# Batch norm with ReLU on one core: regrouping the last two stores so that one of them spans both halves of x

## Chip, cores and metric

One core of a Trainium2 chip; the seven other cores are idle. The metric is the device time of one execution in microseconds (us), as the median of several executions. The span in a profile is about 1.7 us shorter than the time.

## The reference

```python
x: (32, 128, 32, 32) float32      # 16.78 MB in, 16.78 MB out
gamma, beta, running_mean, running_var: (128,) float32

normalized = (x - running_mean[None, :, None, None]) / np.sqrt(running_var[None, :, None, None] + eps)
scaled = normalized * gamma[None, :, None, None] + beta[None, :, None, None]
return np.maximum(scaled, 0).astype(np.float32)
```

## The kernel before

The 4096 (batch, channel) rows of 1024 numbers are dealt out so that a partition holds 16 neighbouring rows of each of two halves (t = 0 and 1). A row is 4 KB, so a partition's part of one half is 64 KB in one piece of HBM. Loads go out on SyncE's queue, stores on ScalarE's (ACT's). One ACTIVATE does one row: relu(scale * x + bias).

```python
TILES = ((0, 0, 2), (0, 2, 4), (0, 4, 8), (0, 8, 16), (1, 0, 16))   # (half, first row, end)
LOAD_CUTS = {(1, 8)}        # the load of the second half is cut at row 8
STORE_CUTS = {(0, 1)}
...
for t, a, b in TILES:
    xt = data.tile([P, b - a, HW], F32, name=f"x{t}_{a}")
    ...                     # one load per piece, all six queued at once
# ... four small loads of the parameters, scale_t and bias_t computed ...
for t, a, b, xt in tiles:
    first = a
    for j in range(a, b):
        nc.scalar.activation(out=xt[:, j - a, ...], in_=xt[:, j - a, ...], func=ACTF.Relu,
                             bias=bias_t[:, j : j + 1], scale=scale_t[:, j : j + 1])
        if j + 1 == b or (t, j + 1) in STORE_CUTS:
            nc.scalar.dma_start(out=outr[t, :, first : j + 1, :], in_=xt[:, first - a : j + 1 - a, :])
            first = j + 1
```

The stores have 0.5, 0.5, 1, 2, 4 and 8 MB. Nothing is written in a buffer twice, so no load waits for a store.

Of the kernel before, what the change touches and what calls it, by code (L numbers as in the profile page):

```python
# [1 line left out]

# [4 lines left out]


F32 = mybir.dt.float32
ACTF = mybir.ActivationFunctionType  # L10



J = 16

TILES = ((0, 0, 2), (0, 2, 4), (0, 4, 8), (0, 8, 16), (1, 0, 16))

LOAD_CUTS = {(1, 8)}
STORE_CUTS = {(0, 1)}

HALVES = {(0, 0), (0, 1)}


@with_exitstack
def kernel(
    ctx: ExitStack,
    tc: tile.TileContext,
    x: bass.AP,
    gamma: bass.AP,
    beta: bass.AP,  # L30
    running_mean: bass.AP,
    running_var: bass.AP,
    eps: bass.AP,
    out: bass.AP,
):
    nc = tc.nc
    B, C, H, W = x.shape
    HW = H * W
    P = nc.NUM_PARTITIONS
    assert C % J == 0 and P % (C // J) == 0 and (B * C) % (P * J) == 0  # L40
    Q = C // J
    T = B * C // (P * J)

    xr = x.rearrange("b c h w -> (b c) (h w)").rearrange("(t p j) w -> t p j w", p=P, j=J)
    outr = out.rearrange("b c h w -> (b c) (h w)").rearrange("(t p j) w -> t p j w", p=P, j=J)

    data = ctx.enter_context(tc.tile_pool(name="data", bufs=1))
    params = ctx.enter_context(tc.tile_pool(name="params", bufs=1))
    psum = ctx.enter_context(tc.tile_pool(name="psum", bufs=1, space=bass.MemoryType.PSUM))

    tiles = []
    for t, a, b in TILES:
        xt = data.tile([P, b - a, HW], F32, name=f"x{t}_{a}")
        cuts = [a] + [j for j in range(a + 1, b) if (t, j) in LOAD_CUTS] + [b]
        for c, d in zip(cuts, cuts[1:]):
            nc.sync.dma_start(out=xt[:, c - a : d - a, :], in_=xr[t, :, c:d, :])  # L56
        tiles.append((t, a, b, xt))



    raw = params.tile([Q, 4, J], F32, name="raw")
    for k, src in enumerate((running_var, gamma, running_mean, beta)):
        nc.scalar.dma_start(out=raw[:, k, :], in_=src.rearrange("(q j) -> q j", j=J))
    eps_t = params.tile([P, 1], F32, name="eps_t")
    nc.vector.memset(eps_t, float(eps))  # L65
    rep = params.tile([Q, P // Q, Q], F32, name="rep")
    nc.gpsimd.memset(rep, 1.0)  # L67
    nc.gpsimd.affine_select(  # L68
        out=rep,
        in_=rep,  # L70
        compare_op=mybir.AluOpType.is_equal,
        fill=0.0,
        base=0,
        pattern=[[0, P // Q], [-1, Q]],
        channel_multiplier=1,
    )
    cols = psum.tile([P, 4, J], F32, name="cols")
    nc.tensor.matmul(  # L78
        cols.rearrange("p k j -> p (k j)"),
        rep.rearrange("q r s -> q (r s)"),  # L80
        raw.rearrange("q k j -> q (k j)"),
        start=True,
        stop=True,
    )
    std_t = params.tile([P, J], F32, name="std_t")
    nc.scalar.activation(out=std_t, in_=cols[:, 0, :], func=ACTF.Sqrt, bias=eps_t[:, 0:1], scale=1.0)  # L86
    rstd_t = params.tile([P, J], F32, name="rstd_t")
    nc.vector.reciprocal(out=rstd_t, in_=std_t)  # L88
    scale_t = params.tile([P, J], F32, name="scale_t")
    nc.vector.tensor_mul(out=scale_t, in0=cols[:, 1, :], in1=rstd_t)  # L90
    ms_t = params.tile([P, J], F32, name="ms_t")
    nc.vector.tensor_mul(out=ms_t, in0=cols[:, 2, :], in1=scale_t)  # L92
    bias_t = params.tile([P, J], F32, name="bias_t")
    nc.vector.tensor_sub(out=bias_t, in0=cols[:, 3, :], in1=ms_t)  # L94

    with tc.manual_schedule(engines={mybir.EngineType.Activation}):
        for t, a, b, xt in tiles:
            first = a
            for j in range(a, b):
                step = HW // 2 if (t, j) in HALVES else HW  # L100
                for w in range(0, HW, step):
                    nc.scalar.activation(  # L102
                        out=xt[:, j - a, w : w + step],
                        in_=xt[:, j - a, w : w + step],
                        func=ACTF.Relu,
                        bias=bias_t[:, j : j + 1],
                        scale=scale_t[:, j : j + 1],
                    )
                if j + 1 == b or (t, j + 1) in STORE_CUTS:
                    nc.scalar.dma_start(  # L110
                        out=outr[t, :, first : j + 1, :], in_=xt[:, first - a : j + 1 - a, :]
                    )
                    first = j + 1


# [1 line left out]
_INS = ['x', 'gamma', 'beta', 'running_mean', 'running_var', 'eps']  # L117
_OUTS = [((32, 128, 32, 32), 'float32')]

_NUMBERS = {'eps': 1e-05}  # L120


# [26 lines left out]
```

## Time and profile before

| | before |
|---|---|
| time, first three runs | 83.94, 83.65, 83.94 us |
| span of the profile | 82.0 us |
| bytes | 33.56 MB, 1792 packets |
| DMA engines busy | 48.7% by loads + 47.6% by stores |
| ACT busy | 39.1 us (48%) |

How to read it: no other part is as busy as the DMA engines. The prediction below shows the strip, the stretches and the order of the issues. One more group of lines, by line and shape, gives what one row costs; its columns are busy us and mean ns, then the idle time before:

```profile
L102 ACT ACTIVATE x<-x,bias_t,scale_t 128x1024 f32<-128x1024 f32 x30 | 34.5, 1227 | 8.5 <-DMA x<-in_x_dram 7.6 <-ACT x L102 0.9
```

ACT's idle time is mostly waiting for loads (7.6 us). ACT keeps up with the loads and isn't the bound.

### The profile page before, as it was taken

What the parts mean: (1) busy time and instruction counts of PE and PEld (TensorE: products, weight loads), DVE (VectorE), ACT (ScalarE), POOL (GpSimd) and SP (SyncE); (2) the same over time, 40 slices, a digit from 0 to 9 for tenths busy, and PEclk for the clock granted to TensorE, in tenths of its full rate; (3) what the DMA queues carried; (4) which work ended last, traced back from release to release, by engine and by line L of the source; (5) the groups of instructions that cost most, each with busy time, mean ns of one, the idle gap of its engine ahead of it and who ended that gap; (6) DMA issues with size and microseconds to landing.
All of it is one profiled execution on the core that took longest, in us unless ns stands there. A gap on an engine that the chain in (4) does not pass through costs nothing.

```text
span 82.0 us, 120 instructions
## 1 busy us (share of the span) xinstructions
PE 0.7 (1%) x2; PEld 0.5 (1%) x2; DVE 0.8 (1%) x5; ACT 39.1 (48%) x36; POOL 0.8 (1%) x6
## 2 busy tenths in 40 slices
PE   0002000000000000000000000000000000000000
PEld 0002000000000000000000000000000000000000
DVE  0000300000000000000000000000000000000000
ACT  0600477799239999199994199993000000000000
POOL 3000000000000000000000000000000000000000
DMA  2899997979899989999799799998992999996590
GB/s 48 336 424 456 416 544 336 524 322 526 338 434 430 506 358 506 390 434 444 320 460 500 316 424 448 512 432 368 480 736 128 416 512 512 512 512 288 224 512 0
DMA packets 1792, 33.56 MB, mean 409 GB/s; under 512 B 256, under 2 KB 256, under 8 KB 512
## 3 DMA queue, kind: packets, MB, share of 16 engines
q1 hardware_dynamic: 864, 16.78, 48.7%
q10 hardware_dynamic: 928, 16.78, 47.6%
HBM read 16.78 MB, written 16.78 MB: 409 GB/s over the span
## 4 chain that ended last, share of the span: by engine, by line
DMA 56%; ACT 10%; issue 2%; SPq 0%
DMA x<-in_x_dram 56%; ACT x L102 10%; SPq L56 0%
## 5 line engine op out<-in xcount | busy, mean ns | idle before, releaser
L102 ACT ACTIVATE x<-x,bias_t,scale_t 128x1024 f32<-128x1024 f32 (+1 forms) x34 | 37.5, 1177 | 9.9 <-DMA x<-in_x_dram 7.6
L86 ACT ACT_TABLE_LOAD x1 | 1.3, 1283 | 2.6 <-issue 2.6
L86 ACT ACTIVATE std_t<-cols,eps_t 128x16 f32<-128x16 f32 x1 | 0.3, 273 | 4.5 <-PE cols L78 4.5
L78 PE MATMUL cols<-raw,rep 8*128 8x64 f32 x2 | 0.7, 429 | 7.6 <-DMA raw<-in_beta_dram 7.6
L78 PEld LDWEIGHTS cols<-raw,rep 8*128 8x128 f32 x2 | 0.5, 306 | 7.6 <-issue 7.6
L68 POOL TENSOR_SCALAR_AFFINE_SELECT rep<-rep 8x128 f32<-8x128 f32 x1 | 0.4, 392 | 0.1
L88 DVE RECIPROCAL rstd_t<-std_t 128x16 f32<-128x16 f32 x1 | 0.3, 254 | 7.7 <-ACT std_t L86 7.7
L67 POOL MEMSET rep<- 8x128 f32 x1 | 0.2, 194 | 0.3 <-POOLq L130 0.3
L90 DVE TENSOR_TENSOR scale_t<-cols,rstd_t 128x16 f32<-128x16 f32 x1 | 0.2, 175 | 0.1
L92 DVE TENSOR_TENSOR ms_t<-cols,scale_t 128x16 f32<-128x16 f32 x1 | 0.2, 175 | 0.0
L94 DVE TENSOR_TENSOR bias_t<-cols,ms_t 128x16 f32<-128x16 f32 x1 | 0.2, 174 | 0.0
L130 POOL MEMSET const-bfloat16-1.0<- 128x1 bf16 x1 | 0.1, 106 | 0.0
L130 POOL MEMSET const-uint8-127<- 128x1 uint8 x1 | 0.1, 106 | 0.0
L130 POOL MEMSET const-float32-0.0<- 128x1 f32 x1 | 0.1, 103 | 0.3 <-issue 0.3
L130 POOL MEMSET const-float32-1.0<- 128x1 f32 x1 | 0.1, 103 | 0.0
L65 DVE MEMSET eps_t<- 128x1 f32 x1 | 0.1, 59 | 0.9 <-PEq L130 0.9
## 6 DMA issues: line engine op xcount, KB each, us to landing
x<-in_x_dram SPq DMA_DIRECT2D x3, 4096.0 KB, 38.7
out_dram<-x ACTq DMA_DIRECT2D x1, 4096.0 KB, 28.7
x<-in_x_dram SPq DMA_DIRECT2D x2, 1024.0 KB, 5.8
x<-in_x_dram SPq DMA_DIRECT2D x1, 2048.0 KB, 11.3
out_dram<-x ACTq DMA_DIRECT2D x1, 2048.0 KB
out_dram<-x ACTq DMA_DIRECT2D x2, 512.0 KB, 19.6
out_dram<-x ACTq DMA_DIRECT2D x1, 1024.0 KB
raw<-in_running_var_dram ACTq DMA_DIRECT2D x1, 0.5 KB
```

Source lines behind the costliest of these rows:

```text
L65: nc.vector.memset(eps_t, float(eps))
L67: nc.gpsimd.memset(rep, 1.0)
L68: nc.gpsimd.affine_select(out=rep, in_=rep, compare_op=mybir.AluOpType.is_equal, fill=0.0, base=0, pattern=[[0, P // Q], [-1, Q]], channel ...
L78: nc.tensor.matmul(cols.rearrange("p k j -> p (k j)"), rep.rearrange("q r s -> q (r s)"), raw.rearrange("q k j -> q (k j)"), start=True, s ...
L86: nc.scalar.activation(out=std_t, in_=cols[:, 0, :], func=ACTF.Sqrt, bias=eps_t[:, 0:1], scale=1.0)
L88: nc.vector.reciprocal(out=rstd_t, in_=std_t)
L90: nc.vector.tensor_mul(out=scale_t, in0=cols[:, 1, :], in1=rstd_t)
L92: nc.vector.tensor_mul(out=ms_t, in0=cols[:, 2, :], in1=scale_t)
L94: nc.vector.tensor_sub(out=bias_t, in0=cols[:, 3, :], in1=ms_t)
L102: nc.scalar.activation(out=xt[:, j - a, w : w + step], in_=xt[:, j - a, w : w + step], func=ACTF.Relu, bias=bias_t[:, j : j + 1], scale=sc ...
L130: nc = _bacc.Bacc("TRN2", target_bir_lowering=False, num_devices=1)
```

## The change

Its intent is to regroup the last 12 MB of stores. Before, rows 8 to 15 of the first half leave in a store of 4 MB, and the whole second half in one of 8 MB. Now one store of 8 MB takes rows 8 to 15 of the first half with rows 0 to 7 of the second, and one of 4 MB the rest. The number of stores stays at six.

```diff
-TILES = ((0, 0, 2), (0, 2, 4), (0, 4, 8), (0, 8, 16), (1, 0, 16))
+TILES = (((0, 0, 2),), ((0, 2, 4),), ((0, 4, 8),), ((0, 8, 16), (1, 0, 8)), ((1, 8, 16),))
...  (tiles get a dimension for their pieces; the same six loads)
+            if len(pieces) == 2:      # after the 16 rows of both pieces
+                (t0, a, b), (t1, c, _) = pieces
+                pitch = ((t1 - t0) * P * J + c - a) * HW
+                nc.scalar.dma_start(
+                    out=bass.AP(
+                        tensor=outr.tensor,
+                        offset=outr[t0, :, a:b, :].offset,
+                        ap=[[J * HW, P], [pitch, 2], [HW, b - a], [1, HW]],
+                    ),
+                    in_=xt,
+                )
```

In HBM the merged store has two runs of 32 KB per partition, 8 MB less 32 KB apart.

More of the change, by code (lines that the diff above doesn't have):

```diff
@@ L14 @@
 J = 16
-TILES = ((0, 0, 2), (0, 2, 4), (0, 4, 8), (0, 8, 16), (1, 0, 16))
-LOAD_CUTS = {(1, 8)}
-STORE_CUTS = {(0, 1)}
+TILES = (((0, 0, 2),), ((0, 2, 4),), ((0, 4, 8),), ((0, 8, 16), (1, 0, 8)), ((1, 8, 16),))
+STORE_CUTS = {(0, 0)}
 HALVES = {(0, 0), (0, 1)}
@@ L51 @@
     tiles = []
-    for t, a, b in TILES:
-        xt = data.tile([P, b - a, HW], F32, name=f"x{t}_{a}")
-        cuts = [a] + [j for j in range(a + 1, b) if (t, j) in LOAD_CUTS] + [b]
-        for c, d in zip(cuts, cuts[1:]):
-            nc.sync.dma_start(out=xt[:, c - a : d - a, :], in_=xr[t, :, c:d, :])
-        tiles.append((t, a, b, xt))
+    for pieces in TILES:
+        n = len(pieces)
+        rows = pieces[0][2] - pieces[0][1]
+        xt = data.tile([P, n, rows, HW], F32, name=f"x{pieces[0][0]}_{pieces[0][1]}")
+        for i, (t, a, b) in enumerate(pieces):
+            nc.sync.dma_start(out=xt[:, i], in_=xr[t, :, a:b, :])
+        tiles.append((pieces, xt))
     raw = params.tile([Q, 4, J], F32, name="raw")
@@ L96 @@
     with tc.manual_schedule(engines={mybir.EngineType.Activation}):
-        for t, a, b, xt in tiles:
-            first = a
-            for j in range(a, b):
-                step = HW // 2 if (t, j) in HALVES else HW
-                for w in range(0, HW, step):
-                    nc.scalar.activation(
-                        out=xt[:, j - a, w : w + step],
-                        in_=xt[:, j - a, w : w + step],
-                        func=ACTF.Relu,
-                        bias=bias_t[:, j : j + 1],
-                        scale=scale_t[:, j : j + 1],
-                    )
-                if j + 1 == b or (t, j + 1) in STORE_CUTS:
-                    nc.scalar.dma_start(
-                        out=outr[t, :, first : j + 1, :], in_=xt[:, first - a : j + 1 - a, :]
-                    )
-                    first = j + 1
+        for pieces, xt in tiles:
+            first = 0
+            for i, (t, a, b) in enumerate(pieces):
+                for j in range(a, b):
+                    step = HW // 2 if (t, j) in HALVES else HW
+                    for w in range(0, HW, step):
+                        nc.scalar.activation(
+                            out=xt[:, i, j - a, w : w + step],
+                            in_=xt[:, i, j - a, w : w + step],
+                            func=ACTF.Relu,
+                            bias=bias_t[:, j : j + 1],
+                            scale=scale_t[:, j : j + 1],
+                        )
+                    if len(pieces) == 1 and (j + 1 == b or (t, j) in STORE_CUTS):
+                        nc.scalar.dma_start(
+                            out=outr[t, :, a + first : j + 1, :], in_=xt[:, 0, first : j + 1 - a, :]
+                        )
+                        first = j + 1 - a
+            if len(pieces) == 2:
+                (t0, a, b), (t1, c, _) = pieces
+                pitch = ((t1 - t0) * P * J + c - a) * HW
+                nc.scalar.dma_start(
+                    out=bass.AP(
[4 more added lines that the diff above has]
+                    in_=xt,
+                )
 _INS = ['x', 'gamma', 'beta', 'running_mean', 'running_var', 'eps']
```

## The prediction

> **What bounds the kernel now.** I read the strip of forty slices and the queue table of the page first, because a kernel that reads 16.78 MB and writes 16.78 MB and does one ACTIVATE per row is probably a copy kernel.
>
> ```profile
> ACT  0600477799239999199994199993000000000000
> DMA  2899997979899989999799799998992999996590
> GB/s 48 336 424 456 416 544 336 524 322 526 338 434 430 506 358 506 390 434 444 320 460 500 316 424 448 512 432 368 480 736 128 416 512 512 512 512 288 224 512 0
> q1 hardware_dynamic: 864, 16.78, 48.7%
> q10 hardware_dynamic: 928, 16.78, 47.6%
> ```
>
> q1 carries the loads, q10 the stores; together they keep the 16 DMA engines busy for 96.3% of 82.0 us, that is 79.0 us. ScalarE (ACT) is busy 48% and has nothing to do for the last 12 slices. The hole at slice 31 (digit 2, 128 GB/s) looks like lost time and has to be checked, for it would lie just where the store of 4 MB hands over to the store of 8 MB. It is not lost: the slice before shows 736 GB/s, far over what any long stretch sustains, and (736 + 128) / 2 = 432. A 64 KB packet is booked whole into one slice. The table of stretches, asked with boundaries of my choice, says the same:
>
> ```profile
> 0.00:2.10 2.10, 0.00 (x0) 0.00 (x0) 0.06 (x1) 0.00 (x0) 0.80 (x6) 1.00 0.27 51
> 2.10:46.70 44.60, 0.66 (x2) 0.50 (x2) 0.78 (x4) 29.91 (x28) 0.00 (x0) 1.00 1.00 424
> 46.70:81.10 34.40, 0.00 (x0) 0.00 (x0) 0.00 (x0) 9.16 (x8) 0.00 (x0) 1.00 0.98 423
> 81.10:82.00 0.90, 0.00 (x0) 0.00 (x0) 0.00 (x0) 0.00 (x0) 0.00 (x0) 1.00 0.00 0
> ```
>
> The last two columns are the DMA share and GB/s. From 2.1 to 81.1 us the share is 1.00 and then 0.98, at 424 and 423 GB/s; before lies the start, after it 0.9 us of end. So the time is 2.1 + 79.0 + 0.9 = 82.0 us, and a reordering of transfers can change it only if it makes the engines idle, makes the bytes slower, or changes the two ends.
>
> Next the order of time, which says when each store is issued:
>
> ```profile
> 21.00 0.34 ACTq L110 DMA_DIRECT2D out_dram<-x  x1
> 23.91 9.16 ACT L102 ACTIVATE x<-x,bias_t,scale_t 128x1024 f32<-128x1024 f32 x8 [2.94 <-DMA x<-in_x_dram]
> 33.10 0.34 ACTq L110 DMA_DIRECT2D out_dram<-x  x1
> 34.85 9.16 ACT L102 ACTIVATE x<-x,bias_t,scale_t 128x1024 f32<-128x1024 f32 x8 [1.78 <-DMA x<-in_x_dram]
> 46.87 9.16 ACT L102 ACTIVATE x<-x,bias_t,scale_t 128x1024 f32<-128x1024 f32 x8 [2.86 <-DMA x<-in_x_dram]
> 56.05 0.34 ACTq L110 DMA_DIRECT2D out_dram<-x  x1
> ```
>
> and the issue list, whose last column is the time from issue to landing:
>
> ```profile
> out_dram<-x ACTq DMA_DIRECT2D x1, 4096.0 KB, 28.7
> out_dram<-x ACTq DMA_DIRECT2D x1, 25.1
> ```
>
> The store of 4 MB is issued at 33.1 and lands 28.7 us after its issue ends, at about 62.1. Its 4.19 MB need only 9.7 us at 432 GB/s, so it begins to move at about 52 us. The packet records of the trace agree: its first packet starts at 51.59, when the 2 MB store ahead of it in the same queue is through, and the next store's first packet starts at 61.28. The store queue has a backlog from its first store to the end. The chain of waits (56% of the span "DMA x<-in_x_dram", then ACT) stops at the issue of the last store and says nothing of this queue; I set no store on it.
>
> **What the Trainium skill says.** "DMA: Bandwidth & Descriptors", section "Queues, rings and completion order", says that each DMA engine takes turns between the queue rows that have work, a whole packet at a time. The trace agrees: from 10 to 46 us the records give the load queue, with packets of 8 to 32 KB, 87.6% of the engines' time and the store queue, with packets of 4 KB for most of it, 12.4%. That is why the early stores take so long: 4 / (4 + 32) is 11%. The two shares sum to 100%, which agrees with the same page's section "Issuing engines are not separate DMA queues". Its section "Why small descriptors are slow" gives a fixed overhead of a few cycles per packet. Here the packet records have a median of 2418 ns for 64 KB and 1213 ns for 32 KB, so one split costs 2 x 1213 - 2418 = 8 ns. The section "Latency and other measured facts" warns that copies with a row pitch of 4 or 8 MiB per partition fell to 103 GB/s, against 207 at 512 KiB. The kernel before has a row pitch of 64 KiB, so its trace doesn't test this; I take it up as a rival.
>
> **The change, part by part.** All six loads keep their sizes, order and semaphore waits (the comparison of instruction order shows 2048, 2048, 4096 and three times 8192 elements per partition on SyncE in both). All 34 ACTIVATEs over x keep theirs. There are six stores in both. What moves:
>
> 1. *Removed: the 4 MB store at 33.10.* ACT loses 0.34 us of issue between two ACTIVATE groups. It lies inside a gap of 1.78 us that ends with a load's landing at 34.85, so ACT starts there at the same time: 0 us.
>
> 2. *Added: one store of 8 MB after the 16 rows that it covers.* It is issued when the group that begins at 34.85 ends, at 34.85 + 9.16 = 44.01, and takes perhaps 0.34 us, in a gap that lasts until the load at 46.87: 0 us for ACT. Its first bytes are available 10.9 us later than the 4 MB store's were. The queue needs them at 51.59. Slack: 51.59 - 44.35 = 7.2 us. The queue doesn't run dry, and the first 4 MB of it move in the same stretch, in packets of the same 32 KB, as the old store's.
>
> 3. *The loads.* They would gain from the missing store only if it competed with them. It does not: the last load packet starts at 45.22 and ends at 46.47 by the records, before any packet of the 4 MB store. Gain: 0 us.
>
> 4. *The last store shrinks from 8 MB to 4 MB.* It is issued at 56.05 as before, since it waits for the same last group. The merged store occupies the queue from 51.59 for 16 packets per engine, 16 x 1.213 = 19.4 us, so to 71.0. Slack: 71.0 - 56.4 = 14.6 us.
>
> 5. *Packets.* 128 packets of 64 KB become 256 of 32 KB: 8 more per engine, 8 x 8 ns = +0.064 us on each engine, and this part is wholly on the path.
>
> 6. *The end.* The last packets of the 16 engines end between 80.59 and 81.10; the engines have fixed shares of partitions, and the offset is already there when the 2 MB store ends (51.59 to 52.10). Smaller packets don't even it out. The 0.9 us after the last data packet belong to one completion and the final barrier, in both: 0 us.
>
> Sum: 0 + 0 + 0 + 0 + 0.06 + 0 = +0.06 us. The three runs before (83.94, 83.65, 83.94) have a mean of 83.84; with 0.06 that is 83.90 us.
>
> **The rivals.** *The store queue runs dry.* If the merged store came after 51.6 us, every microsecond of lateness would be one of idle DMA. With no slack at all, 10.9 us of delay would make about 95 us. What speaks for it: the delay is real. Against: 18 us of waiting in the queue before, and 7.2 us left. It would take a late load, and the loads are the same.
>
> *The merged store moves more slowly.* Its two runs per partition lie 8 MB less 32 KB apart, and each engine would alternate between two far regions. If it fell to half rate, 19.4 us would become 38.8, and the kernel about 103 us. Against: the pitch from partition to partition stays 64 KiB, where the old 4 MB store, with the same 32 KB runs, went at 1213 ns per packet; and the runs are 32 KB long, so the jump is rare. Also, loads and stores interleave in the stretch before, hence distant addresses, at 424 GB/s. A loss of a few per cent of this store (half a microsecond to one) I can't exclude: 84.4 to 84.9.
>
> *Smaller packets change the sharing.* If the store's packets met loads in the queue, smaller ones would get a smaller share. They don't meet: 46.5 against 51.6. And sharing alone loses no time while the engines are full.
>
> *A gain.* Fewer mixed reads and writes, or finer packets that end more evenly, could bring at most the 0.5 us spread of the ends, so 83.4. Part 6 speaks against it.
>
> **Range and chances.** The certain term is 0.06 us and the runs before spread over 0.29 us. Most of the range is the scatter of two medians, plus a little for a slower merged store: 83.5 to 84.4. Faster by over 2% would need 1.7 us out of a DMA stretch that is full: 1%. Slower by over 2% needs the queue to run dry or the merged store to lose 9% of its speed: 2%. Within 2%: 97%.
>
> **What would show it.** In the profile after: two store issues at about 44.0 and 56.05 where before there were 33.1 and 56.05; the landing of the merged store about 71.0 + 0.3 - 44.35, or 27 us after its issue, and of the last one about 25.1; a DMA share of 0.98 to 1.00 from 2.1 to 81.1; 1920 packets instead of 1792, none of 64 KB, all the added ones near 1213 ns; and a span of about 82.1. It would be wrong if a hole stood between 46 and 52 us that neighbouring slices don't make up for (queue dry), if the merged store's packets took longer than 1213 ns (address pattern), or if the load packets ended earlier than 46.47 (competition that I missed).

## The result

The changed kernel takes 83.88 us (83.77 to 84.00, 6 runs), the kernel before 83.71 us (83.54 to 83.94, 6 runs). The ratio is 1.0016, with a 95% interval of 0.9996 to 1.0036: no difference that the runs can tell from none. A ratio here is the mean time of one kernel's fast runs over that of the other's fast runs of the same rounds, so not quite the ratio of the medians quoted.

The profile after, first the strip of DMA and the packet count of the page (span 82.1 us, 40 slices):

```profile
DMA  2899996979799979898799799996998999799690
GB/s 48 351 424 455 407 583 287 529 303 557 305 407 455 525 337 541 353 509 355 327 567 383 315 487 407 511 495 271 511 511 351 415 511 463 303 511 479 287 511 0
DMA packets 1920, 33.56 MB, mean 409 GB/s; under 512 B 256, under 2 KB 256, under 8 KB 512
```

The false hole of before (digit 2 after 736 GB/s) is gone, because the 64 KB packets that made it are gone; what wobbles now does so in pairs that average to the same rate. The stretches, asked with the same boundaries as before (last columns: DMA share, GB/s):

```profile
2.10:46.70 44.60, 0.66 (x2) 0.50 (x2) 0.78 (x4) 29.91 (x28) 0.00 (x0) 1.00 1.01 424
46.70:81.10 34.40, 0.00 (x0) 0.00 (x0) 0.00 (x0) 9.16 (x8) 0.00 (x0) 1.00 0.98 423
```

They repeat those of before to a hundredth, 1.01 for 1.00 in the first apart. The order of time on ACT (start us, us, engine, what):

```profile
34.82 9.16 ACT L104 ACTIVATE x<-x,bias_t,scale_t 128x1024 f32<-128x1024 f32 x8 [1.84 <-DMA x<-in_x_dram]
44.00 0.39 ACTq L120 DMA_DIRECT2D out_dram<-x  x1
46.81 9.16 ACT L104 ACTIVATE x<-x,bias_t,scale_t 128x1024 f32<-128x1024 f32 x8 [2.83 <-DMA x<-in_x_dram]
55.99 0.35 ACTq L112 DMA_DIRECT2D out_dram<-x  x1
```

The issue at 33.10 is gone and one stands at 44.00, in the wait for the last load, where it costs ACT nothing. The issue list (KB, us from issue to landing) shows the two regrouped stores:

```profile
out_dram<-x ACTq DMA_DIRECT2D x1, 8192.0 KB, 27.6
out_dram<-x ACTq DMA_DIRECT2D x1, 4096.0 KB, 25.3
```

The trace also has a record of every DMA packet. By these records the 2 MB store ends between 51.5 and 51.9 us over the 16 engines, and the merged one, though issued at 44.0, sends its first packet at 51.5 on the first engine that is free. Before, the 4 MB store issued at 33.1 sent its first at 51.3. Eleven microseconds of delay in the issue leave the first byte within 0.2 us of where it was.

One warning about these records. The prediction and the expectations quote their times 0.30 us late against the issue times of the same trace: 51.59 us for a packet that starts at 51.29, and likewise for the others. The reading of hold_8 below shows it. Differences between two records are not touched by this; a difference between an issue and a record is. All record times in the rest of this text are on the axis of the issues.

### The profile page after: what moved, and what is told of

Its sections match the earlier page's. It is cut to its first block, busy times and chain, and to the rows that moved or that the text cites. A ratio compares the mean times of both kernels' runs of the same rounds, so it can differ in the third digit from the quotient of the medians.

```text
span 82.1 us, 120 instructions
## 1 busy us (share of the span) xinstructions
PE 0.7 (1%) x2; PEld 0.5 (1%) x2; DVE 0.8 (1%) x5; ACT 39.1 (48%) x36; POOL 0.8 (1%) x6
## 4 chain that ended last, share of the span: by engine, by line
DMA 55%; ACT 10%; issue 2%; SPq 0%
DMA x<-in_x_dram 55%; ACT x L104 10%; SPq L57 0%
```

## The experiments

Two questions are left by a null result. Was the deferral free because of the backlog, or was it a cost that something else paid for? And was the merged layout free? Below, the changed kernel's time in another call is taken as 1.0016 times that of the kernel before in that call. Twelve kernels ran, all correct.

### Packets alone: split_last

```diff
 # kernel before
-STORE_CUTS = {(0, 1)}
+STORE_CUTS = {(0, 1), (1, 8)}
```

> The kernel before, with its last store of 8 MB cut into two of 4 MB (32 KB packets), the first issued after row 7 of the second half. Theory (fed engines, cost of a split 8 ns): 8 more packets per engine, +0.06 us against before, so a ratio of 1.0008, not to be told from 1.000. Rival (smaller packets are what costs, and the deferral gives something back): more than +0.2 us. The packets must show a median of 1213 ns.

Measured: 83.88 us against 83.59, ratio 1.0034 (1.0019 to 1.0049). That is about +0.28 us: the expected 1.0008 lies outside the interval, and the size is the one that the rival named. The packet records have all 384 store packets of 32 KB at a median of 1213 ns. From the completion of the 2 MB store to that of the last one, on the engine that ends first, the records give 29.00 us before, 29.04 in the changed kernel, 29.05 here and 29.00 in the next experiment, which keeps its 64 KB packets. So splitting 64 KB packets costs 0.04 to 0.05 us of store time. The other 0.2 us isn't in the store stretch, and the second half of the rival (the deferral gives something back) has no support in the next experiment. This kernel has a seventh store, and 1.28 us between the last packet and the end of the span instead of 1.17; that may be part of it. The profiled runs can't show the rest, since they hardly differ (83.74 us here, 83.68 before). It stays open.

### Deferral alone: defer_only

```diff
 # kernel before, in the loop over rows
+                if (t, j) == (1, 7):
+                    nc.scalar.dma_start(out=outr[0, :, 8:16, :], in_=tiles[3][3])
-                if j + 1 == b or (t, j + 1) in STORE_CUTS:
+                if (j + 1 == b or (t, j + 1) in STORE_CUTS) and (t, a) != (0, 8):
```

> The kernel before, with the 4 MB store issued at about 44.0 us instead of 33.1 and nothing merged; the last store keeps its 64 KB packets. Theory: the queue has work of its own until 51.6 us, so 0.00 us, ratio 1.000. Rival 1 (the early store helps): slower by some tenths. Rival 2 (the loads run better without it): load packets end before 46.3 us and the time falls by over 0.2 us.

Measured: 83.58 us against 83.59, ratio 1.0007 (0.9989 to 1.0025). The first packet of the deferred store starts at 51.22 us, the last load packet ends at 46.12: both within 0.1 us of before. Deferral from 33.1 to 44.0 costs nothing and gives nothing that the interval of about 0.2% can show.

### A longer deferral: dose_2, dose_5, dose_8

```diff
 # changed kernel; K = 2, 5 or 8; the merged store moves from the end of its tile to a row of the last one
+                    if (t, j) == (1, 8 + K - 1):
+                        nc.scalar.dma_start(out=bass.AP(...as above...), in_=tiles[3][1])
```

> The changed kernel, with the merged store issued only after 2 rows of the last tile, at about 49.1 us. The first store's packets follow its issue by about 1.3 us where the engines are free, so bytes come at 50.4, before 51.6 to 51.8 when the queue runs out. Theory: +0.0 us against the changed kernel (83.9). Rival (the deferral costs in proportion to its length): more time for 5 us more of delay.

> The same after 5 rows of the last tile, at about 52.5 us, bytes at about 53.8. Theory: queue dry for about 2.1 us, so 83.9 + 2.1 = 86.0 us, and a hole at 52 us in the strip. Rival (slack does not matter, only bytes): 83.9.

> The same after all 8 rows of the last tile, at about 56.0 us, bytes at about 57.3. Theory: dry for about 5.6 us, so 89.5 us; against dose_5 the slope is 1 us per us (3 rows, 3.4 us). A smaller slope would say that something else shares the bound.

Measured: 83.63, 83.76 and 83.86 us, against 83.80 for the kernel before; ratios 0.9991, 1.0011 and 1.0012. The expectation of dose_5 and dose_8 failed. Before taking that as a blow to the theory one must look whether the dose was given. The order of time of dose_8:

```profile
46.81 1.24 ACT L104 ACTIVATE x<-x,bias_t,scale_t 128x1024 f32<-128x1024 f32 x1 [2.96 <-DMA x<-in_x_dram]
46.83 0.39 ACTq L114 DMA_DIRECT2D out_dram<-x  x1
47.95 8.01 ACT L104 ACTIVATE x<-x,bias_t,scale_t 128x1024 f32<-128x1024 f32 x7
```

It was not. In the program the issue stands behind all eight rows, but it happens at 46.83, while the first of them runs: ACT's sequencer had handed the rows on and went ahead. In dose_2 it happens at 46.87, in dose_5 at 47.02. "Perfetto Trace Analysis", section "Per-instruction lifecycle: what the profiler-reported window actually captures", has an execution FIFO between sequencer and engine, in which an ACTIVATE waits its turn; this trace agrees: at 46.83 seven rows still waited. One rival is that the compiler had moved the issue forward. The trace speaks against it. Between the end of this issue and the next instruction of ACT's sequencer, the wait before the last store, lie 0.218 us in dose_2, 0.130 in dose_5 and 0.041 in dose_8, where six, three and no rows stand between them in the program: about 0.03 us per row handed on. So the order was the program's. These three runs test only a deferral to about 47, still 4.3 us before the queue needs the store, and there it is free too. To hold a store back, its data must be late.

### Late data: hold_4 and hold_8

Row 7 of the second half, the last row of the merged store, is computed after HOLD rows of the last tile:

```diff
-        (rows 0 to 7 of the second half; merged store; rows 8 to 15; last store)
+        for j in range(0, 7):           row(3, 1, 1, 0, j)
+        for j in range(8, 8 + HOLD):    row(4, 0, 1, 8, j)
+        row(3, 1, 1, 0, 7)
+        (merged store)
+        for j in range(8 + HOLD, 16):   row(4, 0, 1, 8, j)
+        (last store)
```

> dose_2, dose_5 and dose_8 all issued the store at 46.87 us, ahead of the rows that stand before it in the program, since its wait is on its own data alone. So here the data is late: row 7 of the second half, the last row of the merged store, is computed after 4 rows of the last tile, and ends at 46.87 + 5 x 1.145 = 52.6 us. An issue to idle engines took 1.2 us to the first packet (64.43 to 65.60 in late_b), so bytes come at 53.8, and the queue is empty from 51.6 to 52.1. Theory: +1.9 us (1.7 to 2.2) against the changed kernel, about 85.8, and a hole there. Rival (bytes alone count, the slack is not what made the deferral free): 83.9.

> The same after all 8 rows of the last tile: the row ends at 46.87 + 9 x 1.145 = 57.2 us, bytes at 58.4. Theory: +6.5 us (6.3 to 6.8) against the changed kernel, about 90.4; 4.6 us more than hold_4 for 4.6 us more of delay. Rival: less, if anything else fills the hole.

Measured, against 83.70 for the kernel before: hold_4 85.77 us, ratio 1.0237 (1.0207 to 1.0267); hold_8 90.49 us, ratio 1.0807 (1.0778 to 1.0836). Against the changed kernel, 83.83, that is +1.9 and +6.7 us. In hold_8 the order of time has the issue where it was meant to be, and the strip has a real hole (span 88.8 us, so 2.2 us per slice):

```profile
57.34 0.39 ACTq L124 DMA_DIRECT2D out_dram<-x  x1
```
```profile
DMA  2999999979897996979699900099599999599990
GB/s 56 380 422 443 450 495 384 500 297 458 369 502 316 482 531 295 532 303 583 295 417 469 443 30 0 0 472 472 251 458 472 472 472 472 236 472 472 472 472 0
```
```profile
54.00:58.00 4.00, 0.00 (x0) 0.00 (x0) 0.00 (x0) 3.31 (x3) 0.00 (x0) 1.00 0.00 0
52.00:58.50 6.50, 0.00 (x0) 0.00 (x0) 0.00 (x0) 5.30 (x5) 0.00 (x0) 1.00 0.19 81
```

Three slices of 30, 0 and 0 GB/s, with 443 before them and 472 after: no neighbour makes up for them, which is how a real hole differs from the false one of before. By the records the 2 MB store ends between 51.45 and 51.81 over the 16 engines, and the merged store's first packet starts at 58.24, 0.90 us after the issue begins. (The second stretch shows the axis: 81 GB/s over 6.50 us are 0.53 MB, sixteen packets of 32 KB, so the first packet of all 16 engines starts before 58.50. Read 0.30 us late it would start at 58.54.) Hole and lost time agree: 58.24 - 51.6 = 6.6 us. In hold_4 the issue is at 52.85, the first packet at 53.76, and the 2 MB store ends between 51.46 and 52.15: 2.0 us. The 1.2 us from issue to first packet in the expectation is 0.9 on the right axis; its sum comes out the same, since the end of the queue was read as late as the packet. From hold_4 to hold_8 the issue moves by 4.49 us and the time by 4.72. Up to 47.0 us (dose_5), the latest issue tested inside the backlog, a deferral is free; beyond the end of the backlog it costs about one microsecond per microsecond. None of these runs issues it between 47.0 and 52.8 us.

### Far addresses: near_4k and far_4k

Both replace the merged store by eight stores of 1 MB in 4 KB packets, out of a padded tile. near_4k takes two neighbouring rows each time, far_4k one row of either half:

```diff
+# near_4k
+    for i, (t, a, b) in enumerate(pieces):
+        for j in range(a, b, 2):
+            nc.scalar.dma_start(out=outr[t, :, j : j + 2, :], in_=xt[:, i, j - a : j - a + 2, :])
+# far_4k
+    for r in range(b - a):
+        nc.scalar.dma_start(
+            out=bass.AP(tensor=outr.tensor, offset=outr[t0, :, a + r : b, :].offset,
+                        ap=[[J * HW, P], [pitch, 2], [1, HW]]),
+            in_=xt[:, :, r, :])
```

> The changed kernel, the merged store replaced by eight stores of 1 MB, each two neighbouring rows of every partition in 4 KB packets (the tile is padded so that the rows don't join). Theory: 128 packets of 159 ns per engine in place of 16 of 1213: 20.35 - 19.41 = +0.95 us against the changed kernel, so 84.8 us. The eight issues and their waits lie inside the slack. If small packets cost nothing: 83.9.

> As near_4k, but each store takes one row of the first half and one of the second, so the packets of a partition alternate between addresses 8 MB less 32 KB apart, 8 times as often as in the changed kernel. Theory (distance costs nothing here): equal to near_4k within 0.2 us, packets 159 ns. Rival (the distant runs of the merged store cost): packets longer than 159 ns and more time than near_4k; half rate would add 20 us.

Measured: near_4k 85.56 us, ratio 1.0232 (1.0207 to 1.0257); far_4k 85.50 us, ratio 1.0226 (1.0201 to 1.0251); before 83.67. The queues of near_4k, then of far_4k:

```profile
DMA packets 5617, 33.57 MB, mean 400 GB/s; under 512 B 368, under 2 KB 368, under 8 KB 4720
q1 hardware_dynamic: 2656, 16.78, 49.4%
q10 hardware_dynamic: 2960, 16.78, 47.9%
```
```profile
DMA packets 5617, 33.57 MB, mean 399 GB/s; under 512 B 368, under 2 KB 368, under 8 KB 4720
q1 hardware_dynamic: 2656, 16.78, 49.4%
q10 hardware_dynamic: 2960, 16.78, 47.7%
```

The two kernels are equal, and the 4 KB store packets have a median of 159 ns in both: distance costs nothing that shows, though far_4k changes region eight times as often as the changed kernel. Both are 0.7 to 0.8 us slower than expected, and q1 has an explanation. The padded tile cut the two loads into it to 4 KB packets too (2656 packets, not 864), which I had overlooked. Eight 4 KB packets take 8 x 159 - 1213 = 59 ns longer than one of 32 KB. With 16 of those per engine in the stores and 16 in the loads, 32 x 59 ns = 1.9 us are to be expected, and 85.56 - 83.80 = 1.8 are measured (83.80 being 1.0016 x 83.67). That agrees with the price of a packet at a much larger dose: 1.8 us for 224 more packets per engine, or 8 ns each. It doesn't isolate it, because near_4k differs from the changed kernel in more than its packets: the last load packet ends at 53.58 us instead of 46.12, and the last three of the eight store issues took 2.3 to 4.9 us each on ACT's sequencer, which held the last eight rows up:

```profile
48.40 4.89 ACTq L121 DMA_DIRECT2D out_dram<-x  x1
58.54 9.16 ACT L105 ACTIVATE x<-x,bias_t,scale_t 128x1024 f32<-128x1024 f32 x8 [5.64 <-issue]
67.72 0.35 ACTq L113 DMA_DIRECT2D out_dram<-x  x1
```

The last store still came in time, since the queue was through with the eight only at 72.4. far_4k shows nearly the same times (its last eight rows wait 5.64 us too, its last store is issued at 68.01), so the comparison of the two stands.

### Looking for a faster version: late_a, late_b, late_c

The records hint at a loss elsewhere. Load packets of 32 KB exceed their usual 1213 ns by a sum of 0.47 us per engine before, 0.57 after and 0.21 in defer_only, almost all of it after the first store packet. (From run to run this varies: the three dose kernels, with the same loads and early stores as the changed kernel, have 0.38, 0.62 and 0.59.) The three kernels keep stores out of the loads' way.

```diff
 # late_a: changed kernel; the four small stores are issued after row 3 of the second half
+                    if (t, j) == (1, 3):
+                        (the stores of 0.5, 0.5, 1 and 2 MB)
 # late_b: kernel before, one tile and one 8 MB store for each half, the first after row 3 of the second half
+                if (t, j) == (1, 3):
+                    nc.scalar.dma_start(out=outr[0], in_=tiles[0][3])
```

> The changed kernel, with the four small stores held back until row 3 of the second half is done (about 36.5 us). If engines that are full are all that matters, nothing changes: +-0.1 us. If mixing loads and stores costs something (by the median packet times all packets need 77.9 us, the stretch from 2.07 to about 80.85 has 78.8, so 0.9 us are lost somewhere): loads end near 41 us, and the time falls by 0.5 to 0.9 us, to about 83.1. A dry queue would show as more time.

> The kernel before, with one tile for the first half and a single store of 8 MB in 64 KB packets for it, issued after row 3 of the second half; then the last store of 8 MB. Stores need 256 x 2418 ns / 16 = 38.7 us instead of 38.95, loads 38.9. If mixing costs 0.9 us and most of it goes: -0.9 to -1.1 us, about 82.7, and a version faster than both kernels (under 2% though). If mixing costs nothing: -0.25 us. If the stores start later than the loads end: a hole, and no gain.

Measured: late_a 84.44 us, ratio 1.0106 (1.0091 to 1.0121), late_b 88.00 us, ratio 1.0531 (1.0516 to 1.0546), against 83.59. Both expectations missed. late_a's loads do end earlier, at 43.2 us instead of 46.2, but their excess rises to 0.91 us: the same small packets, met in a shorter time, went with more disturbance and not less. (Here too the issues ran ahead, to 32.6 to 34.0 us instead of 36.5; the first store packet starts at 36.5.) late_b shows another thing:

```profile
32.44 0.38 ACTq L110 DMA_DIRECT2D out_dram<-x  x1
33.52 8.01 ACT L102 ACTIVATE x<-x,bias_t,scale_t 128x1024 f32<-128x1024 f32 x7
55.24 9.16 ACT L102 ACTIVATE x<-x,bias_t,scale_t 128x1024 f32<-128x1024 f32 x8 [13.71 <-DMA x<-in_x_dram]
64.43 0.37 ACTq L112 DMA_DIRECT2D out_dram<-x  x1
```

The issue ran ahead again, to 32.4. Its 64 KB packets then took turns with the loads' 32 KB packets, so the stores got two thirds of the engines: from 38 to 53 us the store queue (q10) and the load queue (q1) have:

```profile
q10 hardware_dynamic: 65, 4.26, 65.5%
q1 hardware_dynamic: 65, 2.10, 32.4%
```

The last load, which released ACT at 46.87 before, now does so at 55.24 (idle 13.71 us). The last store goes out only at 64.43, when the queue has been empty since 61.6 to 62.7 us, and its first packet starts at 65.30. Here a store queue with larger packets than the loads starved the loads, and that came back as an empty queue.

late_c ties the first store to late data, as hold_4 does:

```diff
 # late_b, but row 15 of the first half is computed after 5 rows of the second, then the store
+        order = [(0, j) for j in range(15)] + [(1, j) for j in range(5)] + [(0, 15)]
+        order += [(1, j) for j in range(5, 16)]
```

> late_b with the start of its first 8 MB store tied to data: row 15 of the first half is computed after 5 rows of the second, at about 39.3 us, so that 64 KB packets start at about 40.5, when the loads have one packet per engine left or none. Theory: loads end at about 42 to 44, last store issued at about 53 to 54, long before 60, no hole: 77.6 us of packets at their alone durations, +0.5 at the start, instead of 79.0 in all: -0.5 to -0.9 us against before, about 83.0. If loads still starve, or the stores come too late, no gain.

Measured: 83.61 us (83.38 to 84.12, 8 runs) against 83.70, ratio 0.9976 (0.9952 to 1.0001): the same within the interval. The mechanism came as expected. The loads run alone and their excess falls to 0.01 us; the busy time per engine is 78.4 us instead of 79.0. The gain did not come in full: in the profiled run, which at 84.12 us is the slowest of the eight, the engines end 1.1 us apart (79.78 to 80.89) instead of 0.5, 1.5 us instead of 1.2 pass after the last packet, and the 64 KB packets of the stores exceed 2418 ns by a sum of 0.24 us per engine. Why is open. No version clearly beats both kernels.

## Why the prediction was right

Its time was 83.90 us and 83.88 was measured. That the two agree to 0.02 us is luck: the 83.84 from which it started is the mean of three runs, the six have a median of 83.71, and the runs of one kernel spread over 0.2 to 0.4 us. What was right is the sum of free steps, and the result can't tell the 0.06 us from nothing. By its own steps:

1. *Removing the issue at 33.10 is free.* ACT starts the next group at 34.82 for 34.85 before. Right.
2. *The merged store comes early enough, with 7.2 us in hand.* Its issue is at 44.00 for a predicted 44.01. The size is a little off: the queue needed the store at 51.29 in the kernel before and not at 51.59, and the 0.5 us from the end of an issue to the first packet (57.73 to 58.24 in hold_8) were left out, so about 6.4 us were in hand. (Also, the issue list counts a landing from the start of the issue, so the old 4 MB store landed at 33.1 + 28.7 = 61.8, not at 62.1. Nothing rests on it.) The existence of the slack is shown twice: deferral within it changes nothing (defer_only 1.0007, and the three runs with an issue at about 46.9), and beyond it hold_4 and hold_8 lose 1.9 and 6.7 us, within 0.2 us of what the end of the 2 MB store and the delay from issue to first packet give. The first rival, the dry queue, is real but isn't reached. Its figure of 95 us "with no slack" was never put to the test.
3. *The loads gain nothing.* Their last packet ends at 46.12 for 46.17 before. Right.
4. *The last store is early enough.* It is issued at 55.99, and the merged store's packets fill the engines until 70.8 to 71.2. Right; predicted 71.0.
5. *Split packets cost 0.064 us.* On the engine that ends first, the store stretch grew by 0.04 us. The total of near_4k agrees with 8 ns per packet at a dose of 224. Right in kind and close in size; in the total time it is below what the runs resolve.
6. *The ends are as they were.* The last packets end within 0.41 us of each other for 0.51, and 1.18 us follow for 1.17 (the prediction's 0.9 comes from the late axis). Right.

The second rival, a slower merged store, falls: its packets keep a median of 1213 ns, and far_4k equals near_4k. The third, a changed sharing, is real in kind, as late_b shows, but does not occur here, since no packet of a regrouped store meets a load. The prediction's reason that sharing alone loses no time while the engines are full is too strong: in late_a they were shared in another way, and it took about 0.7 us more than the changed kernel, a part of it in longer load packets. The measured ratio of 1.0016 is some 0.13 us, with 0 in its interval. I don't explain more of it than the packets' 0.04. In the two profiled runs the changed one is later by 0.2 us already when the first engine is through with the 2 MB store (51.49 for 51.30), before any regrouped store moves.

## What to carry to other kernels

When the DMA engines are full from end to end, ask of a store not when it is issued but when its queue gets to it: here an issue at 33, 44 or 47 us was the same, and from an issue at 52.85 to one at 57.34 every microsecond counted. A hole in a strip of slices is real only if its neighbours don't exceed the sustained rate. And to hold back an issue on purpose, make its data late; a place behind eight rows of work did not do it here.

## What the Trainium skill lacked or had wrong

- "Perfetto Trace Analysis" has the execution FIFO but no warning: an issue placed behind eight ACTIVATEs on ACT went out at 46.83 us, 9 us before they ended (dose_8). A depth of ScalarE's queue is not lacking in the skill: "TensorE: Matmul & The Clock Gate" has one in its table of figures.
- "DMA: Bandwidth & Descriptors" says that an engine takes turns by packet, and in its section "SWDGE vs HWDGE vs iDMA" has packets of at most 4096 B as the preferred size. Here the trace books each contiguous run as one packet, up to 64 KB (2418 ns), and that decides the sharing: 64 KB stores left 32 KB loads 32.4% of the time, and the last load released ACT 8.4 us later (late_b). The page doesn't draw this consequence.
- The same page gives about 0.6 us to the first byte on these queues, without saying from where it counts. From the start of an issue to the first packet the records show 0.90 us with idle engines, 0.51 us from its end (hold_8), so the figure is not contradicted. What it lacks is the case with loads queued: 3.4 us (first store of the kernel before, 11.16 to 14.60) to 5.0 us (late_b, 32.44 to 37.41).
- The same page's overhead per packet is given in cycles; the packet durations give 8 ns per additional packet; at 8 more per engine the store stretch grew by 5 to 6 ns each, and at 224 more near_4k took 8 ns each.
- The same page's warning about pitches of 4 and 8 MiB doesn't carry over to two runs per partition 8 MB less 32 KB apart: 85.50 us far against 85.56 near. The pitch between partitions was 64 KiB in both, so the warning itself was not tested.
- No page has the cost of interleaving loads and stores: 0.2 to 1.2 us per engine here, summed over the 32 KB load packets (1.2 in late_b), 0.01 where the loads ran alone (late_c), not explained. In near_4k the last 32 KB loads met 4 KB stores with an excess of only 0.02, which belongs to what is open.
